# Delta-rule scan of a diffusion layer: two interleaved recurrences against one joint recurrence

## The chip, the cores and the metric

The kernel runs on one core of one Trainium2 chip, in one launch. The metric is the device time of that launch in microseconds (us); of several runs the median is taken. Four engines matter here: TensorE (PE, matmuls, with weight loads PEld beside them), VectorE (DVE), ScalarE (ACT), and the SyncE queue (SP) that issues most transfers. [...]

## The reference

One layer of a diffusion backbone over 512 latent tokens with 256 context tokens ahead, width 1024. A norm and one input projection feed two mixers, window attention and a bidirectional gated delta rule; their outputs are gated, summed, projected and added to the input, and an MLP follows. The change lies in the delta rule alone. Per direction (forward and backward in time), with 8 heads of 64 and chunks of 64 tokens:

```python
w_mat = triangular_solve(t_mat, (bc * eG)[..., None] * kc, ...)
u_v = triangular_solve(t_mat, bc[..., None] * vc, ...)
intra = dec_incl * jnp.einsum('bhnid,bhnjd->bhnij', qc, kc)
q_dec = eG[..., None] * qc
k_tail = jnp.exp(g_last[..., None] - G)[..., None] * kc

def step(S, xs):
    w_c, uv_c, qd_c, intra_c, kt_c, gl_c = xs
    u = uv_c - jnp.einsum('bhck,bhkv->bhcv', w_c, S)
    o = jnp.einsum('bhck,bhkv->bhcv', qd_c, S) + jnp.einsum('bhij,bhjv->bhiv', intra_c, u)
    S = jnp.exp(gl_c)[..., None, None] * S + jnp.einsum('bhck,bhcv->bhkv', kt_c, u)
    return S, o
...
return o_f + flip(o_b), s_f, s_b
```

The context has 4 chunks and the latents 8. The context scan starts from zero, its states start the latent scan, and its outputs are not used.

## The kernel before, in words

Everything is fp32. Large matrices are split into a high and a low part (`split`, and lines 271 and 276 for weights: ACT makes the high part, DVE the low one), and each product is three fp32r matmuls of 128x512. The scan's own products are small plain fp32 matmuls, 64x64 by 64 columns, four of them side by side in quarters of the array. The profile counts each of these as two records.

The scan is slow in latency and small in work, so large products are laid between its pieces. They come from a generator `fill` (432 products of 128x512: eight tiles of `br_a`, line 1086, then gate tiles of `gate_tiles`, line 1040; each tile is a group in one PSUM bank that ACT drains at its end, through the helper at line 164 or at 1088). `run_fill(n)` lays n of them at a place, and `FILL` holds the counts. The program's order is only a priority: a planner puts each engine's instructions into a fixed order when the kernel is built, from its own estimate of when each becomes ready, so a product that is not ready in its estimate lets later ones pass. On the chip each engine then works strictly in that order, with semaphores for the dependencies.

`chain_step(d, step)` is one step of one direction. Its state `state[d]` is [128 x 256]: two heads on the two halves of the partitions, four pairs side by side. `zb[d]` is one pair of PSUM banks per direction, in which all products of that direction lie. A step has three pieces, and `steps` runs each piece for d = 0, then d = 1, and then yields:

1. state products, line 1156: k·S and, in the latents, q·S (32 records of each kind for the two directions together); then on DVE R = eG·(k·S) (line 1160) and R = -0.5·v + R (line 1161).
2. u = X·R, line 1175, where X is the inverse of the triangular matrix; DVE makes `uk` = tb·u (line 1181), the decay and beta on the key side; in the latents ACT copies u (`us`, line 1185) and makes `zq` = eG·(q·S), in four pieces of 64 columns (line 1187).
3. k·uk, line 1195, into the same banks; ACT scales the old state in four pieces (`se`, line 1205), DVE makes the new state `se` - k·uk (line 1206; line 1200 in the first step); in the latents IA·us (line 1213), and DVE adds up the output (line 1218 in the first half of the steps, 1220, 1221, 1223 and ACT's square 1222 in the second half).

With `FILL[3] = (8, 7, 3)`, 8 large products follow piece 1, 7 piece 2 and 3 piece 3 in the latent scan.

The stages around it, in order of time in the profiled run:

- the context scan (about 290 to 348 us): the four context steps are woven with the inversion of the latents' triangular matrices on DVE (lines 864 and 865), 144 large products, and `rest()` (norm of q, line 676, and the token-major copies of k and v of the latents: `to_tokens`, four TensorE transposes at line 923 and ACT copies of 64x256 at line 928).
- the stage between the scans (about 348 to 398 us): the latents' inverses are completed (`combine`, lines 885 to 909), and the masked q·k blocks `IA` are made (line 786, DVE 1293 to 1296, ACT 1302 to 1305; `qq` takes two banks), with large products and with 12 pieces of `late_mod` between them: each loads 512 KB (`wada2`, line 1104) and reduces it on DVE (line 1105).
- the latent scan (about 398 to 470 us), with four more pieces of `late_mod`, each in a buffer that is taken for it from the arena.
- then the output norm of the scan (lines 1336 and 1341), the last gate tiles, the projections and the MLP.

Buffers in SBUF come from one arena of 167 units that is handed out in turn, so where a buffer lies, and what it has to wait for, depends on all that was taken before.

Of the kernel before, what the change touches and what calls it, by code (L numbers as in the profile page):

```python
# [20 lines left out]
FILL = 144, 28, 36, (8, 7, 3)  # L21
# [91 lines left out]
def tile_layer(ctx: ExitStack, tc: tile.TileContext, I: dict, out: bass.AP, dbg=None):  # L113
# [37 lines left out]
    bc = lambda ap, n: ap.unsqueeze(2).broadcast_to([ap.shape[0], ap.shape[1], n])  # L151

# [591 lines left out]
    eg = const.tile([P, 5, NM], F32, name="eg")  # L744
    eG, tb, tbO = eg[:, 0:2], eg[:, 2:4], eg[:, 4]
# [8 lines left out]
    act(eg[:, 0:5].rearrange("p n m -> p (n m)"), egp[:, :5 * NM], AF.Exp)  # L754
# [158 lines left out]
    def strided(ap, *dims):  # L913

        return bass.AP(ap.tensor, ap.offset, [list(ap.ap[0]), *map(list, dims)])

    def tok_major(src, dst, cs, places):

        hi, lo = (places[2] ^ places[0], places[1] ^ places[0])
        for c0 in cs[::2]:  # L920
            pt = bank()
            for q in range(4):
                PE.transpose(pt[:, q * P:(q + 1) * P], src[q][:, col(c0):col(c0) + P], ident)
            for i in range(2):
                o = (c0 + i - cs[0]) * 256
                for a in range(2):
                    sg = 64 - 128 * a
                    A.activation(dst[64 * a:64 * a + 64, o:o + 256].rearrange("p (x y f) -> p x y f", x=2, y=2),  # L928
                                 strided(pt[64 * i:64 * i + 64, 64 * a:512], (256 + sg * hi, 2), (128 + sg * lo, 2), (1, 64)), AF.Copy)
            pt.free()  # L930

    KTM, VTM = [None] * 3, [None] * 3
# [79 lines left out]
    def to_tokens(dst, src, g):  # L1012
        dst[g] = alloc(1024, True)
        tok_major(src, dst[g], range(4 * g, 4 * g + 4), ZP if dst is VTM else UP)
# [77 lines left out]

    for q in range(4):
        silu2(qT[q].ap, qT[q].ap)
# [5 lines left out]
    def late_mod(grp):  # L1100

        for j in range(8):
            wa = alloc(1024)
            nc.sync.dma_start(out=wa.ap, in_=I["wada2"][grp, j])
            V.scalar_tensor_tensor(wa.ap, wa.ap, 0.5, scr.ap, op0=ALU.mult, op1=ALU.mult, accum_out=modT[:, grp, j:j + 1])  # L1105
            wa.free()
            if j == 7:
                V.tensor_tensor(modT[:, grp], modT[:, grp], bada[:, 16 + 8 * grp:24 + 8 * grp], op=ALU.add)
            yield

    late = (x for grp in range(4) for x in late_mod(grp))
# [20 lines left out]
    hv = lambda ap: ap.rearrange("p (q v) -> p q v", q=4)  # L1132
    state = [None, None]
    zb = [bank(2), bank(2)]
    Sb = [[alloc(256), alloc(256)] for _ in range(2)]

    def chain_step(d, step):
        lat = step >= NCC
        c = step if d == 0 else NC_ - 1 - (step - NCC) if lat else NCC - 1 - step
        cl = c - NCC if lat else c  # L1140
        S, last = state[d], step == NC_ - 1
        m4 = slice(c * 4, c * 4 + 4)
        z = zb[d]
        r2 = [slice(0, 64), slice(64, 128)]
        vt = VTM[c // 4][:, c % 4 * 256:(c % 4 + 1) * 256]

        zt = z.ap.rearrange("p (b n) -> p b n", b=2)
        by2 = lambda ap: ap.rearrange("p (b n) -> p b n", b=2)
        hv2 = lambda ap: ap.rearrange("p b (q v) -> p b q v", v=HD)
        bc2 = lambda ap: ap.rearrange("p (b q) -> p b q", b=2).unsqueeze(3).broadcast_to([P, 2, 2, HD])  # L1150
        if S is not None:
            for x, src in enumerate((kT, qT) if lat else (kT,)):
                for q in (0, 2, 1, 3):
                    for a in range(2):
                        o = 512 * ZP[q] + 128 * x + 64 * (q % 2)
                        PE.matmul(z[r2[a ^ ZP[q]], o:o + HD], src[q][r2[a], col(c):col(c) + CH],
                                  S[r2[a], SPOS[q] * HD:(SPOS[q] + 1) * HD], start=True, stop=True)
            Rb = alloc(256)
            R = Rb.ap
            V.tensor_tensor(hv2(by2(R)), hv2(zt[:, :, 0:128]), bc2(eG[:, d, m4]), op=ALU.mult)  # L1160
            V.scalar_tensor_tensor(R, vt, -0.5, R, op0=ALU.mult, op1=ALU.add)
        else:
            R = vt
        yield
        u = zt[:, :, 256:384]

        def place(q):

            o = 512 * (UPOS[q] // 2) + 256 + 64 * (UPOS[q] % 2)
            return slice(o, o + HD)  # L1170

        for q in (0, 1, 3, 2):
            for a in range(2):
                r = r2[a ^ ZP[q]]
                PE.matmul(z[r2[a ^ UP[q]], place(q)], XA[lat][d][r, (cl * 4 + q) * CH:(cl * 4 + q + 1) * CH],
                          R[r, q * HD:(q + 1) * HD], start=True, stop=True)
        if S is not None:
            Rb.free()
        if not last:
            uk = alloc(256)  # L1180
            V.tensor_tensor(hv2(by2(uk.ap)), hv2(u), bc2(tb[:, d, m4]), op=ALU.mult)
        if lat:
            us, zqb = alloc(256), alloc(256)
            zq = zqb.ap
            A.activation(by2(us.ap), u, AF.Copy)
            for q in range(4):
                A.activation(zq[:, UPOS[q] * HD:(UPOS[q] + 1) * HD], zt[:, ZP[q], 128 + 64 * (q % 2):192 + 64 * (q % 2)], AF.Copy,
                             scale=eG[:, d, c * 4 + q:c * 4 + q + 1])
        yield
        if not last:  # L1190
            sn = zt[:, :, 384:512]
            for q in range(4):
                for a in range(2):
                    r, o = r2[a ^ UP[q]], 512 * UP[q] + 384 + 64 * (q // 2)
                    PE.matmul(z[r2[a], o:o + HD], KTM[c // 4][r, (c % 4 * 4 + q) * HD:(c % 4 * 4 + q + 1) * HD],
                              uk[r, UPOS[q] * HD:(UPOS[q] + 1) * HD], start=True, stop=True)
            uk.free()
            Sn = Sb[d][step % 2]
            if S is None:
                V.tensor_scalar(by2(Sn.ap), sn, 0.5, None, op0=ALU.mult)  # L1200
            else:
                se = alloc(256)
                for q in range(4):
                    o = slice(SPOS[q] * HD, (SPOS[q] + 1) * HD)
                    A.activation(se[:, o], S[:, o], AF.Copy, scale=egl[:, d, c * 4 + q:c * 4 + q + 1])
                V.tensor_tensor(by2(Sn.ap), by2(se.ap), sn, op=ALU.subtract)
                se.free()
            state[d] = Sn
        if lat:
            for q in (0, 1, 3, 2):  # L1210
                for a in range(2):
                    r = r2[a ^ UP[q]]
                    PE.matmul(z[r2[a ^ ZP[q]], place(q)], IA[d][r, (cl * 4 + q) * CH:(cl * 4 + q + 1) * CH],
                              us[r, UPOS[q] * HD:(UPOS[q] + 1) * HD], start=True, stop=True)
            us.free()
            dst = ot_[:, cl * 256:(cl + 1) * 256]
            if step - NCC < NCL // 2:
                V.tensor_tensor(by2(dst), by2(zq), u, op=ALU.add)
            else:
                V.tensor_tensor(by2(zq), by2(zq), u, op=ALU.add)  # L1220
                V.tensor_tensor(dst, dst, zq, op=ALU.add)
                A.activation(zq, dst, AF.Square)
                V.tensor_reduce(oss[:, cl], hv(zq), axis=AX.X, op=ALU.add)
            zqb.free()

    def steps(r):
        for step in r:
            both = [chain_step(d, step) for d in range(2)]
            for _ in range(3):
                for g in both:  # L1230
                    next(g, None)
                yield

    def rest():
        for q in range(4):
            l2n(qT[q].ap, HD ** -0.5, ((0, SEQ),), epsc4)
            yield
        for g in (1, 2):
            to_tokens(VTM, vT, g)
            yield  # L1240
        for t in vT:
            t.free()
        for g in (1, 2):
            to_tokens(KTM, kT, g)
            yield

    to_tokens(VTM, vT, 0)
    to_tokens(KTM, kT, 0)
    weave((steps(range(NCC)), 3 * NCC), (inv, 40), (fill, FILL[0]), (rest(), 9))
    for _ in inv:  # L1250
        pass
    for b in KTM[:1] + VTM[:1] + XA[0]:
# [59 lines left out]

    ot_ = alloc(2048, True)
    ot = ot_.ap.rearrange("p (c q v) -> p c q v", c=NCL, q=4)
    for n, _ in enumerate(steps(range(NCC, NC_))):
        run_fill(FILL[3][n % 3])
        if n % 3 == 1 and n < 3 * NCL // 2:
            run_late(1)
    for _ in fill:
        pass  # L1320
    for b in kT + qT + KTM[1:] + VTM[1:] + XA[1] + IA + zb + Sb[0] + Sb[1]:
# [362 lines left out]
def pack(i):  # L1684
# [45 lines left out]
    for n, (kind, places, order) in enumerate(((0, ZP, range(4)), (1, ZP, range(4)), (0, UP, UORD), (1, UP, UORD), (0, (0,) * 4, range(4)))):  # L1730
# [27 lines left out]
```

## Time and profile before

| | us |
|---|---|
| median of 3 runs | 913.39 (912.81 to 914.12) |
| the profiled execution | 911.42 |
| span of its profile | 909.7 |
| TensorE busy in it | 873.9 (96%) |
| VectorE busy | 652.9 (72%) |
| ScalarE busy | 496.9 (55%) |

The span runs from the first to the last instruction; 1.7 us of the execution lie outside it. TensorE's matmuls overlap each other, so its busy time is the time in which at least one runs, and the mean duration of a matmul is not what the next one waits.

### The profile page before, as it was taken

The page shows a single profiled execution, that of the slowest core. Times are in us where ns is not written, and L with a number is a line of the kernel's source. Part 1 is how long each engine was busy: PE and PEld are TensorE (multiplying, and loading weights), DVE is VectorE, ACT ScalarE, POOL GpSimd, SP SyncE. Part 2 cuts the span into 40 slices and gives each one's busy share as a digit, 9 for nine tenths or more (in the row PEclk, how much of TensorE's full clock was granted, in tenths as well). Part 3 has the DMA queues.
Part 4 walks back from the last instruction along what each step waited for, and adds up shares of the span by engine and source line. Part 5 has one row for each costly group of instructions (what it writes and reads, how often), then busy time and mean ns, then how long its engine had stood idle before and what let it go on. Part 6 is the DMA issues. An engine that isn't in the chain of part 4 may idle for free.

```text
span 909.7 us, 18033 instructions
## 1 busy us (share of the span) xinstructions
PE 873.9 (96%) x7564; PEld 721.3 (79%) x7564; DVE 652.9 (72%) x1111; ACT 496.9 (55%) x881; POOL 26.0 (3%) x42
## 2 busy tenths in 40 slices
PE   8999999989999998889999999999999999999998
PEld 6688667867777676656677789888898899889986
DVE  5665799876778999566666968896587567837631
ACT  6368764475768795475654434463265246424520
POOL 0000001010000001100000000000000000000000
PEclk9999999999999999999999999999999999999999
DMA  9824455532311136523143645453412332334031
GB/s 355 312 76 117 94 131 107 113 73 47 57 36 35 59 121 235 182 67 99 49 152 107 241 127 186 155 170 115 139 48 93 116 116 70 116 93 139 1 116 46
DMA packets 31985, 107.13 MB, mean 118 GB/s; under 512 B 4000, under 2 KB 4512, under 8 KB 31904
## 3 DMA queue, kind: packets, MB, share of 16 engines
q1 hardware_dynamic: 29600, 97.59, 32.1%
q0 software_dynamic: 2304, 8.39, 5.8%
q8 instruction: 59, 0.97, 0.4%
q14 instruction: 22, 0.18, 0.1%
HBM read 103.87 MB, written 2.10 MB: 116 GB/s over the span
## 4 chain that ended last, share of the span: by engine, by line
PE 60%; DVE 20%; ACT 11%; DMA 6%; issue 3%; SPq 0%; ACTq 0%; DVEq 0%
PE banks L293 12%; PE banks L294 12%; PE banks L295 12%; PE banks L1509 11%; PE banks L1040 5%; DMA m<-in_wada 3%; ACT m L164 2%; DVE m L865 2%; DVE m L864 2%; DVE m L1105 2%; DVE m L204 2%; DMA m<-in_wm 1%; DVE wl L276 1%; ACT m L928 1%; DVE m L875 1%
## 5 line engine op out<-in xcount | busy, mean ns | idle before, releaser
L293 PE MATMUL banks<-m,wh 128*128 128x512 f32 (+1 forms) x568 | 213.2, 376 | 0.5 <-ACT m L203 0.5
L294 PE MATMUL banks<-m,wh 128*128 128x512 f32 (+1 forms) x568 | 210.7, 371 | 0.3 <-DVE m L204 0.2
L295 PE MATMUL banks<-m,wl 128*128 128x512 f32 (+1 forms) x568 | 209.8, 370 | 0.0
L271 ACT ACTIVATE wh<-wr 128x1024 fp32r<-128x1024 f32 (+1 forms) x92 | 90.6, 987 | 130.5 <-PE banks L294 102.5
L1509 PE MATMUL banks<-m,m 128*128 128x256 f32 x1008 | 123.2, 284 | 0.9 <-ACT m L203 0.6
L1509 PEld LDWEIGHTS banks<-m,m 128*128 128x128 f32 x1008 | 121.9, 192 | 2.4 <-ACT m L203 1.2
L203 ACT ACTIVATE m<-m 128x512 fp32r<-128x512 f32 (+2 forms) x118 | 81.9, 719 | 75.0 <-DVE m L1487 12.0
L293 PEld LDWEIGHTS banks<-m,wh 128*128 128x128 f32 x568 | 107.0, 189 | 19.2 <-ACT m L203 1.0
L294 PEld LDWEIGHTS banks<-m,wh 128*128 128x128 f32 x568 | 107.0, 188 | 18.8 <-DVE m L204 1.2
L295 PEld LDWEIGHTS banks<-m,wl 128*128 128x128 f32 x568 | 106.9, 188 | 18.6 <-issue 0.7
L1040 PE MATMUL banks<-m,wh 128*128 128x512 f32 x320 | 108.2, 409 | 3.5 <-ACT m L164 3.5
L204 DVE TENSOR_TENSOR m<-m,m 128x512 fp32r<-128x512 f32 (+2 forms) x118 | 92.3, 804 | 22.3 <-ACT m L203 14.1
L276 DVE TENSOR_TENSOR wl<-wr,wh 128x1024 fp32r<-128x1024 f32 (+1 forms) x76 | 84.2, 1110 | 14.9 <-ACT wh L271 12.6
L1636 DVE SCALAR_TENSOR_TENSOR m<-banks,modT,m 128x512 f32<-128x512 f32 x32 | 24.0, 750 | 68.6 <-PE banks L295 68.4
L1040 PEld LDWEIGHTS banks<-m,wh 128*128 128x128 f32 x320 | 59.6, 190 | 16.5 <-ACT m L164 4.0
L1040 PE MATMUL banks<-m,wl 128*128 128x512 f32 x160 | 65.5, 410 | 0.0
L1105 DVE SCALAR_TENSOR_TENSOR m<-m,m 128x1024 f32<-128x1024 f32 x32 | 38.8, 1220 | 14.3 <-DMA m<-in_wada 14.2
L293 PE MATMUL banks<-m,m 128*128 128x256 f32 (+1 forms) x136 | 44.9, 344 | 1.4 <-ACT m L300 1.2
L294 PE MATMUL banks<-m,m 128*128 128x256 f32 (+1 forms) x136 | 45.1, 340 | 0.9 <-DVE m L301 0.8
L295 PE MATMUL banks<-m,m 128*128 128x256 f32 (+1 forms) x136 | 44.6, 337 | 0.0
L164 ACT ACTIVATE m<-banks,st 128x512 f32<-128x512 f32 (+1 forms) x32 | 23.5, 738 | 24.7 <-DVE st L570 24.4
L1040 PEld LDWEIGHTS banks<-m,wl 128*128 128x128 f32 x160 | 30.5, 190 | 6.5
(258 smaller groups left out, 1339.5 us busy)
## 6 DMA issues: line engine op xcount, KB each, us to landing
m<-in_wada SPq DMA_DIRECT2D x48, 512.0 KB, 5.3
wr<-in_wm SPq DMA_DIRECT2D x40, 512.0 KB, 3.6
wr<-in_win SPq DMA_DIRECT2D x39, 512.0 KB, 3.7
m<-in_wm SPq DMA_DIRECT2D x24, 512.0 KB, 3.9
wl<-in_win POOLq DMA_DIRECT2D x16, 512.0 KB, 5.6
m<-in_xT SPq DMA_DIRECT2D x8, 512.0 KB, 5.6
wr<-in_wbr SPq DMA_DIRECT2D x16, 256.0 KB, 2.6
wr<-in_wout SPq DMA_DIRECT2D x8, 512.0 KB, 3.8
```

The source lines that it names most:

```text
L164: r = A.activation(out_, in_, func, **kw)
L203: A.activation(r32(hi), src, AF.Copy)
L204: (eng or V).tensor_tensor(r32(lo), src, hi, op=ALU.subtract)
L271: upper[0] = A.activation(r32(hi), raw, AF.Copy)
L276: V.tensor_tensor(r32(lo), raw, hi, op=ALU.subtract)
L293: PE.matmul(acc, w[0][:, k, :], xhi, start=(start and i == 0), stop=False)
L294: PE.matmul(acc, w[0][:, k, :], xlo, start=False, stop=False)
L295: r = PE.matmul(acc, w[1][:, k, :], xhi, start=False, stop=(stop and i == n - 1))
L1040: PE.matmul(acc.ap, w[x][:, k, :], hx[k][y], start=(k == p == 0), stop=(k == KT - 1 and p == 2))
L1105: V.scalar_tensor_tensor(wa.ap, wa.ap, 0.5, scr.ap, op0=ALU.mult, op1=ALU.mult, accum_out=modT[:, grp, j:j + 1])
L1509: PE.matmul(dst, r32(self.w[w][i][:, k * P:(k + 1) * P]), xs7[x][k][j], start=(n == 0), stop=(n == 11))
L1636: V.scalar_tensor_tensor(xn_[ct], accs[ct].ap, modT[:, 3, ct:ct + 1], xn_[ct], op0=ALU.mult, op1=ALU.add)
```

## The change

Both directions become one recurrence, with 512 columns where there were 256.

- `scan_step` takes the place of `chain_step`: each product is issued for both directions, then one DVE or ACT instruction works on both. The state is one [128 x 512] buffer.
- The banks of the scan go by kind of product: a pair for k·S, a pair for u and the k·u products, and in the latent scan a third pair for q·S and the intra products. That is six banks in the latent scan, where there were four.
- tb (decay and beta of the key side) is multiplied into the token-major keys ahead of the scan: `k_tokens` makes a forward and a backward copy of each group of four chunks, each by one DVE multiply of 128x1024. So `uk` is gone; ACT's copy `us` of u is now made in every step and is what the k·u product reads.
- The 0.5 of v goes into the copies of v (`tok_major(..., scale)`); the output sums of a step (`sums`) are put off to the next step, behind its R. q·S moves behind u. `se` is made ahead of u; in the latents the backward half of it by one DVE multiply.
- The keys' copies for the latents move from the context scan into the stage between the scans (one group in each of the two `IA` rounds). The latents' v copies now come first in `rest()`.
- eG is written in the order of the steps (three small ACT exponentials in place of a part of one).
- The `late_mod` pieces of the latent scan share one buffer (`lbuf`); a few buffers are freed half way through the scan. `FILL[3]` is (8, 3, 7).

The core of the diff:

```diff
-FILL = 144, 28, 36, (8, 7, 3)
+FILL = 144, 28, 36, (8, 3, 7)
...
+    def k_tokens(g):
+
+        kf, kb = alloc(1024, True), alloc(1024, True)
+        tok_major(kT, kb, range(4 * g, 4 * g + 4), UP)
+        kv = lambda b: b.ap.rearrange("p (n f) -> p n f", f=HD)
+        for d, dst in ((0, kf), (1, kb)):
+            V.tensor_tensor(kv(dst), kv(kb), bc(tb[:, d, 16 * g:16 * g + 16], HD), op=ALU.mult)
+        KTM[g] = kf, kb
...
         for j in range(8):
-            wa = alloc(1024)
+            wa = lbuf[0] if lbuf else alloc(1024)
...
+    def sums(step, cl, zq, o):
...
+        if step - NCC < NCL // 2:
+            V.tensor_tensor(dst, by_d(b2(zq.ap)), by_d(o), op=ALU.add)
+        else:
+            V.tensor_tensor(b2(zq.ap), b2(zq.ap), o, op=ALU.add)
+            V.tensor_tensor(dst, dst, by_d(b2(zq.ap)), op=ALU.add)
+            A.activation(by_d(b2(zq.ap)), dst, AF.Square)
+            V.tensor_reduce(...)
+
+    def scan_step(step):
...
+        if S is not None:
+            with_state(kz, kT)
+            Rb = alloc(512)
+            V.tensor_tensor(heads(b2(Rb.ap)), heads(kz[:, :, 0:256]),
+                            eGs[:, step]..., op=ALU.mult)
+            V.tensor_tensor(rv, rv, strided(v0, (128, 2), (vstep, 2), (1, 128)), op=ALU.subtract)
...
+        for f in later:
+            f()
+        later.clear()
+        if S is not None and not last:
+            se = alloc(512)
+            for d in range(1 + (not lat)):
+                for q in range(4):
+                    A.activation(se[:, o:o + HD], S[:, o:o + HD], AF.Copy, scale=egl[...])
+            if lat:
+                V.tensor_tensor(half(se.ap), half(S.ap), strided(egl[...]), op=ALU.mult)
         yield
+        for d in range(2):
+            ... PE.matmul(uz[...], XA[lat][d][...], R(d, q)[r], start=True, stop=True)
+        us = alloc(512)
+        A.activation(b2(us.ap), uz[:, :, 0:256], AF.Copy)
         if lat:
+            oz, zq = b2(zb[2].ap), alloc(512)
+            with_state(oz, qT)
+            for d in range(2):
+                for q in range(4):
+                    A.activation(zq[...], oz[...], AF.Copy, scale=eGs[...])
         yield
         if not last:
+            ... PE.matmul(uz[r2[a], UP[q], o:o + HD], KTM[cs2[d] // 4][d][r, k0:k0 + HD], u_(d, q)[r], ...)
+            Sn = Sb[step % 2]
+                V.tensor_tensor(b2(Sn.ap), b2(se.ap), uz[:, :, 256:512], op=ALU.subtract)
+        yield
         if lat:
+            ... PE.matmul(oz[r2[a ^ ZP[q]], b, 256 + o:256 + o + HD], IA[d][...], u_(d, q)[r], ...)
+            later.append(lambda: sums(step, cl, zq, oz[:, :, 256:512]))
...
     for g in range(2):
...
         run_late(LATE)
+        k_tokens(1 + g)
         run_fill(FILL[2] - FPAUSE)
```

More of the change, by code (lines that the diff above doesn't have):

```diff
@@ L1109, in late_mod @@
             yield
+    lbuf = []
     late = (x for grp in range(4) for x in late_mod(grp))
@@ L1131, in tile_layer @@
     oss = small([P, NCL, 4], "oss", bufs=1)
-    hv = lambda ap: ap.rearrange("p (q v) -> p q v", q=4)
-    state = [None, None]
+    state = [None]
     zb = [bank(2), bank(2)]
[L1135 to L1152, printed above, removed]
+    Sb = [alloc(512), alloc(512)]
@@ L1167, in place @@
[L1167 to L1176, printed above, removed]
+                        o = 128 * d + 64 * (q % 2)
+                        so = 256 * UP[q] + 128 * d + 64 * (q // 2)
@@ L1189, in chain_step @@
         yield
         if not last:
[L1191 to L1198, printed above, removed]
+            for d in range(2):
+                for q in range(4):
+                    for a in range(2):
+                        r, o = r2[a ^ UP[q]], 256 + 128 * d + 64 * (q // 2)
+                        k0 = (cs2[d] % 4 * 4 + q) * HD
+                        PE.matmul(uz[r2[a], UP[q], o:o + HD], KTM[cs2[d] // 4][d][r, k0:k0 + HD], u_(d, q)[r], start=True, stop=True)
@@ L1207, in chain_step @@
                 se.free()
-            state[d] = Sn
+            state[0] = Sn
+        yield
         if lat:
[L1210 to L1224, printed above, removed]
+            for d in range(2):
+                for q in (0, 1, 3, 2):
+                    for a in range(2):
+                        r, (b, o) = r2[a ^ UP[q]], place(d, q)
+                        PE.matmul(oz[r2[a ^ ZP[q]], b, 256 + o:256 + o + HD], IA[d][r, (cl[d] * 4 + q) * CH:(cl[d] * 4 + q + 1) * CH],
+                                  u_(d, q)[r], start=True, stop=True)
@@ L1226, in steps @@
+            later.append(lambda: sums(step, cl, zq, oz[:, :, 256:512]))
+        us.free()
     def steps(r):
         for step in r:
[L1228 to L1232, printed above, removed]
+            yield from scan_step(step)
     def rest():
+        yield from v_tokens(range(NCC, NC_))
+        for t in vT:
+            t.free()
+        yield
         for q in range(4):
@@ L1237, in rest @@
             yield
[L1238 to L1249, printed above, removed]
+    for _ in v_tokens(range(NCC)):
+        pass
+    k_tokens(0)
+    weave((steps(range(NCC)), 3 * NCC), (inv, 40), (fill, FILL[0]), (rest(), 7))
     for _ in inv:
         pass
-    for b in KTM[:1] + VTM[:1] + XA[0]:
+    for b in [*KTM[0], VTM[0], *XA[0]]:
         b.free()
@@ L1311, in tile_layer @@
     dump("qT0", qT[0].ap)
+    for b in kT:
+        b.part(SEQ, CTX).free()
+    lbuf.append(alloc(1024))
     ot_ = alloc(2048, True)
-    ot = ot_.ap.rearrange("p (c q v) -> p c q v", c=NCL, q=4)
+    zb.append(bank(2))
+    first = [b.part(1024 * d, 1024) for bs in (XA[1], IA) for d, b in enumerate(bs)] + [KTM[1][0], KTM[2][1]]
     for n, _ in enumerate(steps(range(NCC, NC_))):
+        if n == 3 * NCL // 2:
+            for b in first:
+                b.free()
         run_fill(FILL[3][n % 3])
```

102 lines of the change are left out of this document (64 added, 38 removed).

## The prediction

> **What bounds the kernel now.** I read the page's busy times first, then the busy time by stage, then, for the latent scan alone, the groups by line and shape, the waits, and TensorE's timeline.
>
> ```profile
> span 909.7 us, 18033 instructions
> PE 873.9 (96%) x7564; PEld 721.3 (79%) x7564; DVE 652.9 (72%) x1111; ACT 496.9 (55%) x881; POOL 26.0 (3%) x42
> ```
>
> TensorE is busy nearly always: 909.7 - 873.9 = 35.8 us is all that filled gaps could ever give. By stage (context scan, the stage between, latent scan, the rest; columns are length, then busy time of PE, PEld, DVE, ACT, POOL):
>
> ```profile
> 290.00:348.00 58.00, 55.02 (x557) 41.16 (x556) 54.90 (x104) 47.39 (x107) 2.07 (x4) 0.97 0.29 92
> 348.00:398.00 50.00, 43.60 (x970) 33.83 (x968) 34.91 (x58) 26.98 (x49) 5.76 (x12) 1.00 0.56 191
> 398.00:470.00 72.00, 66.58 (x1319) 46.97 (x1319) 45.73 (x105) 45.94 (x156) 0.46 (x1) 1.00 0.22 69
> 470.00:910.00 440.00, 432.58 (x2511) 381.99 (x2510) 298.40 (x440) 186.75 (x258) 0.00 (x0) 1.00 0.36 119
> ```
>
> The change's own stages leave 3.0, 6.4 and 5.4 us of TensorE idle. In the context scan DVE is 95% full, in the latent scan neither DVE nor ACT is (64% each). So instructions saved on them don't count there by their busy time, only by what TensorE waits for. But busy time hides a second loss. The latent scan, line by line:
>
> ```profile
> L1040 PE MATMUL banks<-m,wh 128*128 128x512 f32 x90 | 33.0, 420 | 0.0
> L1040 PE MATMUL banks<-m,wl 128*128 128x512 f32 x45 | 19.1, 425 | 0.0
> L1187 ACT ACTIVATE m<-banks,eg 128x64 f32<-128x64 f32 x64 | 15.0, 339 | 0.0
> L1156 PE MATMUL banks<-m,m 64*64 64x64 f32 x448 | 10.0, 223 | 0.7 <-DVE m L1218 0.4 <-DVE m L1220 0.2
> L1195 PE MATMUL banks<-m,m 64*64 64x64 f32 x224 | 9.3, 230 | 1.6 <-ACT m L1187 1.2
> L1175 PE MATMUL banks<-m,m 64*64 64x64 f32 x256 | 7.2, 229 | 2.7 <-DVE m L1161 2.5
> L1213 PE MATMUL banks<-m,m 64*64 64x64 f32 x256 | 6.7, 226 | 0.4 <-DVE m L1206 0.4
> L1160 DVE TENSOR_TENSOR m<-banks,eg 128x256 f32<-128x256 f32 x15 | 6.3, 419 | 1.1 <-PE banks L1156 1.1
> L1206 DVE TENSOR_TENSOR m<-m,banks 128x256 f32<-128x256 f32 x14 | 5.8, 419 | 12.8 <-PE banks L1195 10.8 <-ACT m L1187 1.9
> L1105 DVE SCALAR_TENSOR_TENSOR m<-m,m 128x1024 f32<-128x1024 f32 x3 | 3.7, 1226 | 2.7 <-DMA m<-in_wada 2.7
> L1296 DVE TENSOR_TENSOR m<-m,banks 128x512 f32<-128x512 f32 x1 | 0.7, 689 | 0.0
> ```
>
> That is 135 large products and 448 + 224 + 256 + 256 = 1184 records of small ones. Their undisturbed pace stands in the chain of work just after the scan, and in TensorE's timeline (start, length):
>
> ```profile
> 469.79 9.75 PE banks L1040 x42
> ```
>
> ```profile
> 398.15 0.46 PE L1175 MATMUL banks<-m,m 64*64 64x64 f32 x16
> ...
> 440.75 0.97 ACT L1187 ACTIVATE m<-banks,eg 128x64 f32<-128x64 f32 x4
> 441.17 1.05 PE L1195 MATMUL banks<-m,m 64*64 64x64 f32 x32
> 442.16 0.50 PE L1040 MATMUL banks<-m,wl 128*128 128x512 f32 x1
> 442.59 0.69 PE L1213 MATMUL banks<-m,m 64*64 64x64 f32 x32
> 443.21 0.73 PE L1040 MATMUL banks<-m,wh 128*128 128x512 f32 x2
> 444.36 1.02 PEld L1156 LDWEIGHTS banks<-m,m 64*64 64x64 f32 x64 [0.39 <-DVE m L1220]
> ...
> 446.03 0.62 PE L1040 MATMUL banks<-m,wh 128*128 128x512 f32 x2
> ...
> 469.10 0.69 PE L1213 MATMUL banks<-m,m 64*64 64x64 f32 x32
> ```
>
> A large product every 9.75/42 = 0.232 us, a small record every 1.02/64 = 0.016 us. 135 x 0.232 + 1184 x 0.016 = 31.3 + 18.9 = 50.2 us, and the stage is 72. Of the other 21.8 us the named waits of TensorE are 2.5 + 1.2 + 0.4 + 0.4 + 0.2 = 4.7. The rest is mostly the change between large and small products. Take the group at 442.59: from the large product ahead of it to the one behind it 443.21 - 442.16 = 1.05 us, less one product (0.232) and 32 records (0.51): 0.31 us; and the pair behind it took 0.73, where the pair at 446.03, with large ones around it, took 0.62. I call it 0.4 us a group, an estimate. From 398.15 to 469.10 I count 36 such groups in the timeline: 14.4 us. The remaining 2.7 us are stalls inside groups, like the 1.05 us at 441.17 for 32 records that take 0.69 two lines below: its second half waited for ACT's zq pieces (440.75, 0.97 us, so until 441.72).
>
> **The change part by part.**
>
> Groups in the latent scan. As programmed both kernels have three groups of small products a step: k·S behind the intra products of the step before, u (with q·S in the new one), and k·u. The old one ran 36 in 8 steps, 4.5 a step, because products of one direction weren't ready and large ones passed. In the new one all products of a group become ready by one instruction for both directions. At best 8 x 3 = 24 are left (-12 x 0.4 = -4.8 us), at worst 36 (0). I take 28, nearer to the best, since the pieces' readiness is now common but q·S and the intra products still have conditions of their own: -8 x 0.4 = **-3.2 us**.
>
> Waits in the latent scan. (a) L1195 waits for L1187, which reads other columns of the same banks, so the order is kept by bank; k·u therefore waited for all of zq. With q·S in a third pair this is gone: 1.2 us named, and 0.36 inside a group in up to 7 steps, 3.7 us at most. (b) L1175 <- L1161, 2.5 us: DVE's R. Part of it is R queued behind L1105, which itself waits for its transfer (2.7 us in this stage). The shared buffer lets each of those transfers start as soon as the one before is used, a step earlier; I credit half, 1.2. (c) New: R of both directions is now two instructions in a row. 256 columns take 419 ns, 512 take 689 (L1296), so R is ready 2 x 0.69 = 1.4 us after k·S, with about 0.1 for the hand-over; behind k·S lie 8 large products, 1.86 us, and half a change. That covers it by about 0.5 us while DVE is free, and not when a 1.23 us instruction (such as L1105) has just begun: then 0.6 us is bare. Say in two of eight steps, 1.2 us. (d) New: q·S must wait until the output sum of the step before has left the third pair of banks; that is one DVE instruction of 0.69 behind R, while u's group lasts 0.51: 0.2 x 8 = 1.6 us. What is queued behind q·S on TensorE is the large products and k·u. The new state (0.69 us on DVE, and 0.42 less for `uk` ahead of it) lies behind 7 products and the intra group, 2.1 us. Sum: -3.7 - 1.2 + 1.2 + 1.6, about **-2.0 us**; between -6 (all waits gone, 4.7 named and part of the stalls) and +3 (c bare in every step).
>
> [...]
>
> Context scan. TensorE's waits there include u's consumer:
>
> ```profile
> PE banks L1195 <- DVE m L1181: 1.7, 2, 1.2
> PE banks L1040 <- ACT m L164: 2.9, 2, 2.3
> L928 ACT ACTIVATE m<-banks 64x256 f32<-64x256 f32 x48 | 18.1, 377 | 0.6
> L1088 ACT ACTIVATE m<-banks 128x512 f32<-128x512 f32 x8 | 4.7, 586 | 0.0
> ```
>
> (the first two rows are of the waits from 290 to 480 us, the others of the groups from 290 to 500). k·u no longer waits for DVE, whose queue held the inversion and transposes, but for an ACT copy of about 0.59 us (L1088). 1.7 us can go; ACT's own queue may take some of it: -1.2. DVE: of 27 instructions of 0.42 (11.3 us) become 6 for R and 4 for the state of 0.69 (6.9) and 2 key multiplies of about 1.23 (2.5, by L1105's width): -1.9 us of a full engine, but TensorE has only 3.0 us idle here and large products to run. ACT loses 16 of the 48 copies at L928 (-6.0) and gains four of `us` (+2.4). I take **-1.2 us**, between -3.0 and +1.
>
> The stage between. It takes in what the context scan loses: the keys' 16 transposes and 16 copies (6.0 us of ACT), and 4 key multiplies (4.9 us of DVE), behind `late_mod` on DVE. ACT's queue matters for one reason: the 2.9 us of L1040 <- L164 (longest 2.3) is a gate tile that wants a bank which ACT has not drained, because ACT was making IA:
>
> ```profile
> 391.31 0.41 ACT L1305 ACTIVATE m<-m 32x256 f32<-32x256 f32 x1
> 391.75 1.06 ACT L271 ACTIVATE wh<-wr 128x1024 fp32r<-128x1024 f32 x1
> 392.71 0.58 ACT L164 ACTIVATE m<-banks 128x512 f32<-128x512 f32 x1
> 393.34 0.72 PE L1040 MATMUL banks<-m,wh 128*128 128x512 f32 x2 [2.30 <-ACT m L164]
> ```
>
> The scan then holds four banks, `qq` two, and two are left; the transposes want one of these as well. Nothing to +2 x 3.0 us (ACT's copies ahead of a drain, once a round); nearest is one wait like the 2.3. I take **+1.7 us**. TensorE's share of the move costs nothing, the same 16 transposes leave the stage before.
>
> Small things. The last step's sums come behind the scan at 512 columns. L1336 is what the first output transpose waits for, after 42 large products that hide most of it; +0.3 (0 to +1). The three exponentials for eG, well before the scan, and the subtraction in place of L1161 at equal width: 0. Buffers move in the arena for the whole of the rest (432.58 of 440 us busy, so little to win): 0, ±1.5.
>
> Sum: -3.2 - 2.0 - 1.2 + 1.7 + 0.3 = **-4.4 us**. The profiled execution took 911.42 us (1.7 more than its span), 2.0 below the median 913.39; a stage's saving is the same in both, so 913.4 - 4.4 = **909.0 us**.
>
> **The rivals.**
>
> Lockstep (slower). Two recurrences covered each other: while DVE made R of one, TensorE had the other's products. Now every wait is common to both. Place: u's group behind R, in 11 steps. Price: when DVE is taken at the end of k·S, 0.6 us; with sums, splits and `late_mod` crowding into the same gaps, 0.6 us in each of 11 steps (6.6) and some 1.4 at the new state: -4.4 + 8 = +3.6, 917 us. It decides from the point where R comes later than 1.86 + 0.2 us after k·S in most steps. Against it: DVE's share in the latent scan falls (two of 256 cost 0.84, one of 512 0.69, and `uk` goes). For it: DVE's 95% in the context scan. Chance 0.18.
>
> Banks (no change). The wait for drained banks that costs 2.3 us once now comes in each IA round, and the scan keeps six banks, two for the gate tiles. +6 in place of +1.7: -0.1, 913 us. Against it in the scan itself: a tile of 24 products spans 24/135 of 72 us, 13 us, far longer than any stretch of ACT. Chance 0.17.
>
> [...]
>
> The planner splits the groups as before (gain without its first term): -4.4 + 3.2 = -1.2, 912.2 us. The groups at 1195 stood split with nothing but its estimate as a reason, and it still has conditions for q·S and IA. Chance 0.15.
>
> All of it works: 24 groups and nearly all named waits gone, -4.8 - 4.5 and the stage between for nothing: about -9, 904.4 us. Chance 0.08.
>
> **How the numbers follow.** The forecast has 0.42, with its own range 905 to 912. About 0.2% (1.8 us) is what a measurement can tell from no change. Faster by more: 0.39 of the forecast, all of the last rival 0.08, 0.06 of the split groups, 0.06 of the banks: 0.59. Within: 0.02, 0.07, 0.06 and 0.01 of lockstep: 0.16. Slower: 0.25, which is lockstep's 0.17, the bad ends of banks and split groups, and misplaced buffers. Range for 8 in 10: from 904, which takes in most of the full gain, to 917, lockstep's middle.
>
> **What the changed profile would show.** Right: the latent scan about 67 us in place of 72, some 28 groups of small products in it, no wait of k·u for zq; 512-column DVE instructions near 0.69 us, and `us` near 0.59; the stage between 1 to 2 us longer, with ACT ahead of the gate tile's drain. Wrong: u waiting for R in most steps (lockstep); L1040's successor waiting for drains by more than 5 us (banks); 36 groups again. A gain or a loss outside 290 to 480 us would be the arena's.

## The result and the profile after

The joint recurrence is slower: 916.66 us (median, 912.69 to 922.13) against 913.14 (911.01 to 915.10) for the kernel before, a ratio of 1.004, 95% interval 1.0027 to 1.0053. The forecast was 909.0. The profiled execution took 916.27 us, 4.85 more than that of before.

The top of the page after:

```profile
span 914.5 us, 17917 instructions
PE 869.9 (95%) x7564; PEld 720.8 (79%) x7564; DVE 650.3 (71%) x1053; ACT 492.7 (54%) x850; POOL 26.1 (3%) x42
```

TensorE has 4.0 us less busy time than before and the span is 4.8 us longer, so 8.8 us more of it is idle. The same four windows as in the prediction say where to look:

```profile
290.00:348.00 58.00, 53.38 (x548) 39.36 (x548) 53.22 (x92) 44.68 (x97) 0.00 (x0) 1.00 0.31 94
348.00:398.00 50.00, 41.86 (x873) 32.92 (x871) 38.62 (x57) 31.13 (x56) 7.27 (x14) 0.93 0.57 191
398.00:470.00 72.00, 66.72 (x1452) 50.34 (x1442) 43.38 (x69) 43.16 (x129) 1.04 (x2) 1.00 0.24 75
470.00:914.00 444.00, 432.67 (x2505) 381.24 (x2503) 298.09 (x437) 185.38 (x256) 0.00 (x0) 1.00 0.36 117
```

In the latent scan TensorE is as busy as before (66.72 against 66.58) but runs 1452 records in place of 1319. The rest, which the change does not touch, is 4 us longer for the same busy time (432.67 against 432.58). To put times on this I compared the start of the k-th matmul that uses all 128 rows (4508 of them in both traces), after minus before. Between 300 and 470 us the two kernels run these matmuls in different orders, so single values mean nothing there:

| about (us) | 30 to 290 | 476 | 515 | 685 | 755 | 784 | 850 | 881 |
|---|---|---|---|---|---|---|---|---|
| after is late by | 2.3 | -1.4 | -1.4 | 0.6 | 1.1 | 4.0 | 4.8 | 4.9 |

Most of the first 2.3 us arise at 20 us, in a part that is the same in both (a stretch of half clock, see the last section). Between 290 and 515 us the change gains 3.7 us (2.3 + 1.4). Then 6.3 us are lost behind the scan (1.4 + 4.9), nearly all of it in the MLP. TensorE's largest waits from 640 us on, before and then after (the columns are total, times, longest):

```profile
PE banks L1509 <- ACT m L203: 0.6, 1, 0.6
PE banks L1509 <- DVE m L204: 0.3, 1, 0.3
PE banks L294 <- DVE m L204: 0.2, 1, 0.2
```

```profile
PE banks L1552 <- ACT m L207: 3.0, 4, 1.0
PE banks L297 <- ACT m L1563: 1.4, 1, 1.4
PE banks L1552 <- DVE m L208: 1.1, 2, 0.8
```

Lines 1509 and 1552 are the same products of the MLP. And the chain of waits in the worst place (start, length, what), before, where it is TensorE alone, and after:

```profile
751.89 16.20 PE banks L1509 x135
```

```profile
754.94 3.20 PE banks L1552 x26
758.14 0.02 issue
758.16 3.51 DMA m<-in_wm
761.67 0.02 issue
761.69 0.63 ACT m L207
...
765.17 1.46 ACT m L207 x2
766.63 0.49 ACT m L1563
...
767.16 0.50 PE banks L297
```

By this chain a transfer of raw MLP weights could start only at 758.14, when a product had read the buffer whose place it takes. The transfer took 3.51 us, the row of ACT's instructions behind it another 5.4 (761.69 to 767.12), and the product that needs them came late: from 755 to 785 us TensorE is busy for 27.73 of 30 us, before for all 30. The queue that issues these transfers shows it too, its waits for those products, before and after:

```profile
SPq L1482 <- PE banks L1509: 42.5, 7, 11.6
```

```profile
SPq L1525 <- PE banks L1552: 51.4, 13, 9.9
```

Why do places differ so far behind the scan? One cause is a buffer that is never given back. The context scan advances the generator of steps exactly 3 x 4 times; `scan_step` has code behind its third yield (`us.free()`), which the old step piece did not need for its last piece. So the 512-column `us` of the last context step holds two of the arena's 167 units to the end, and all that is taken later lies elsewhere.

### The profile page after: what moved, and what is told of

It is laid out like the page before. It is cut to its first block, busy times and chain, and to the rows that moved or that the text cites. A ratio compares the mean times of both kernels' runs of the same rounds, so it can differ in the third digit from the quotient of the medians.

```text
span 914.5 us, 17917 instructions
## 1 busy us (share of the span) xinstructions
PE 869.9 (95%) x7564; PEld 720.8 (79%) x7564; DVE 650.3 (71%) x1053; ACT 492.7 (54%) x850; POOL 26.1 (3%) x42
```

## The experiments

Theory A: the change gains in the scan, and the places of the buffers behind it cost more. Theory B: the scan itself, or the half clock, makes the kernel slower. Line numbers differ by a few between the kernels; in the runs with the places set by hand, the products of the MLP are lines 1563 and 1518, and line 1510 where two units are held.

**Scan and places crossed.** The new scan with the places of before, from the output projection on:

```diff
+    ctx_steps = steps(range(NCC))
-    weave((steps(range(NCC)), 3 * NCC), ...)
+    weave((ctx_steps, 3 * NCC), ...)
+    for _ in ctx_steps:
+        pass
...
-    Y = [alloc(1024) for _ in range(8)]
+    Y = [mem.claim(s, 1024) for s in (99, 103, 107, 115, 135, 139, 143, 147)]
+    mem.ptr = 151
```

(`claim` takes a buffer at a given unit; two earlier groups of buffers keep off these units.) The old scan with the places of after:

```diff
-    Y = [alloc(1024) for _ in range(8)]
+    mem.claim(34, 512)
+    Y = [mem.claim(s, 1024) for s in (80, 84, 88, 92, 96, 105, 115, 135)]
+    mem.ptr = 139
```

By the traces, TensorE, VectorE and ScalarE have from about 540 us on the order of instructions of the kernel whose places were given. The orders of before and after differ up to about 860 us, so in these runs the places bring their order with them.

> The changed kernel with two edits: the 512-column buffer that its context scan never hands back is handed back, and from the output projection on every buffer lies where the kernel before has it, so that the order of instructions there is the one of before. Theory A (the loss is made behind the scan, by where buffers lie and the order that follows from it; the scan itself gained): the MLP stage takes what it took before, the lead of some 3.7 us that the profile shows at the end of the scan stays, about 909 us (907 to 911). Theory B (the joint recurrence is slower in itself, or keeps TensorE's clock down): about 916 us as the changed kernel, and the MLP stage as long as in it.

> The mirror of the run above: the kernel before with its own scan, but from the output projection on with the buffers of the changed kernel, the two lost units included, and so with its order of instructions. Theory A: the MLP stage loses the 6 us or so that it loses in the changed kernel, about 919 us (917 to 921). Theory B: no change, 913 us.

Measured: the first 909.90 us, ratio to before 0.997 (0.9956 to 0.9984); the second 919.88, ratio 1.0087 (1.0056 to 1.0119). As a table of medians, with 912.41 for before in the first of these runs:

| | places of before | places of after |
|---|---|---|
| old scan | 912.4 | 919.9 |
| new scan | 909.9 | 916.7 |

The places cost 7.5 us with the old scan and 6.8 with the new one; the new scan gains 2.5 with the old places and 3.2 with the new ones. The 916.7 comes from other rounds, with 913.1 for before beside it; by the ratios the places cost 7.9 and 6.4 us, and the scan gains 2.7 and 4.3. The waits from 640 us on go with the places and not with the scan; first the new scan with old places, then the old scan with new ones:

```profile
PE banks L1563 <- ACT m L214: 1.2, 1, 1.2
PE banks L1563 <- DVE m L215: 0.3, 1, 0.3
```

```profile
PE banks L1518 <- ACT m L210: 3.4, 4, 1.0
PE banks L300 <- ACT m L1529: 1.4, 1, 1.4
PE banks L1518 <- DVE m L211: 1.1, 2, 0.9
```

That settles it for A: a loss larger than the gain, behind the scan, from the places and the order of instructions that the planner makes from them. How much of it is late transfers and how much is the other order, these runs do not show.

Theory B keeps a small part. The granted clock of every run is on record: its mean is 0.9916 over the 12 runs of the new scan with the old places, and 0.9950 over the 23 of before beside them. Within one kernel, a run whose clock is lower by 0.001 takes about 0.5 us longer (all runs taken together), so by this estimate some 1.8 us of the new scan's gain are lost again to half clock. The old scan with the new places has 0.9928, too near to 0.9950 to make its 7.5 us.

**The buffer alone.** The new kernel with that one buffer handed back (the first part of the diff above and nothing else), and the kernel before holding 512 columns that it does not use (`alloc(512)` behind the context scan):

> The changed kernel, with only the lost 512-column buffer handed back; all places behind it move, to yet another pattern. Theory A: the scan's lead stays and the MLP stage is any of the patterns: between 909 and 917 us, another time than 916.7 by more than 1 us. Theory B: 916.7 us within 1 us.

> The kernel before, with a 512-column buffer taken behind the context scan and never given back: nothing is computed with it, only places move. Theory A: another pattern behind the scan, so the time moves by more than 1 us, rather up (913 to 920 us). Theory B: 913 us within 1 us.

Measured: 912.79 us, ratio 1.000 (0.9985 to 1.0015), and 925.84, ratio 1.0148 (1.0123 to 1.0173). Handing it back wins 3.9 of the 6.8 us. The places are then neither those of before nor those of after, because the scan's other buffers differ too; that the rest comes from these is likely and was not tried. Holding two units costs the old kernel 13.4 us, with nothing of the scan changed:

```profile
PE banks L1510 <- ACT m L203: 7.1, 5, 3.1
```

```profile
SPq L1483 <- PE banks L1510: 92.3, 12, 18.2
```

Part of the 13.4 us is clock: this trace has 10.2 us of half clock in the MLP's stretch (755.8 to 759.2 and 854.8 to 861.6 us), where the trace of before has none; that is worth at most 5.1 us. The size of the loss is not a matter of how much memory is held: two units, 1.2% of the arena, move the old kernel by 13.4 us and the new one by 3.9.

**The scan itself.** The base is the new scan with the old places (909.90). Its trace shows three things to try: ACT's scaled old state waits 3.0 us for a place that DVE has just used; u waits for R 7 times, 5.1 us in all, of which 4 times and 2.7 us lie in the latent scan; the keys' transposes compete for two banks in the stage between. Four edits:

```diff
-            se = alloc(512)
+            if step == NCC:
+                se, mem.ptr = mem.claim(52, 512), 41
+            else:
+                se = alloc(512)
```

> Base: the new scan with the places of before behind it (909.9 us in its runs, 2.5 below before). There ACT's first copy of the latent scan, the scaled old state, waits 3.0 us for DVE's last modulation product, because its buffer lies on units 39 and 40 and that product's transferred rows lie on 37 to 40; the drain of a gate tile queued behind it comes late, TensorE waits 3.6 us for the drain, and a stretch of half clock (6.83 us) follows. This kernel gives that one buffer units 52 and 53, free since the stage before; nothing else moves. Theory A (places make waits inside the stage between the scans too): both waits go and perhaps the half clock with them, -2 to -6 us on the base, a ratio to before of 0.991 to 0.995. Theory B (the stage is bound by its transposes and the two banks left, the wait only shows where): another wait takes its place, within 1 us of the base, 0.996 to 0.998.

Measured: 911.81 us, ratio 0.9985 (0.9971 to 0.9998). A falls, and the time lies above B's range too. The wait of 3.6 us fell to 1.9, and another grew in the same stage from 1.3 to 6.4, the keys' transposes for the drained `qq`:

```profile
PE banks L934 <- DVE m L1341: 6.4, 1, 6.4
```

```diff
-FILL = 144, 28, 36, (8, 3, 7)
+FILL = 144, 28, 36, (8, 7, 3)
```

> Base as for e5. The large products between the groups of a latent step go back from 8, 3, 7 to 8, 7, 3: seven behind u, three behind the new state's products. Theory A (the waits decide, as the forecast's step on the new state has it): ACT's copy of u needs no more than 0.6 us and had cover enough with three; the new state (0.69 us on DVE, with the hand-over about 1 us) now has three products (0.70) and the intra group (0.5) as cover in place of seven and is bare by 0 to 0.4 us in up to 7 steps: +0.5 to +3 us on the base, ratio to before 0.998 to 1.001. Theory B (the number of groups decides, and the planner places the large products by its own costs): the number stays near 25 and the time within 1 us of the base, 0.996 to 0.998.

Measured: 910.19, ratio 0.9967 (0.9951 to 0.9983): B. Which of these two gaps is filled makes no difference that shows here.

The same line with (10, 3, 5):

> Base as for e5. Ten large products behind k.S in place of eight, five behind the new state in place of seven. In the base u waits for R 7 times, 5.1 us in all, 1.1 at most. Theory A (R of both directions is too long for eight products: the forecast's step c, bare in nearly every step rather than in two of eight): two more products are 0.46 us a step, u's wait falls to about 2 us and the new state is still covered: -2 to -3.5 us on the base, ratio to before 0.993 to 0.995. Theory B (the two products are missed elsewhere, the new state or the intra group becomes late by as much): within 1 us of the base, 0.996 to 0.998.

Measured: 907.93, ratio 0.9938 (0.9918 to 0.9958): at the edge of A's range. In the latent scan u's wait fell from 2.7 us to 1.6. (The expectation of (12, 3, 3) below sets 1.6 beside 5.1, which are of different stretches: over both scans it is 4.1 beside 5.1, and the context scan's part does not change.) So the wait gives 1.1 of the 2 to 3 us that were won.

```diff
-            later.append(lambda: sums(step, cl, zq, oz[:, :, 256:512]))
+            sums(step, cl, zq, oz[:, :, 256:512])
```

> Base as for e5. The output sums of a latent step are issued right behind its intra products, not behind the R of the step after. Theory A (order on DVE decides: the sum waits for the intra products and stands ahead of R): R comes later by the sum's 0.69 us in up to 7 steps, u waits by as much more, +2 to +5 us, ratio to before 0.999 to 1.003. Theory B (the planner puts R ahead anyway, or q.S gains what R loses, since the third pair of banks is drained sooner): within 1 us of the base, 0.996 to 0.998.

Measured: 910.20, ratio 0.9965 (0.9950 to 0.9980): B. Putting the sums off gains nothing that shows.

**Four more: the stage between, the scan's fill, and both.** First the keys of both rounds ahead of the first `qq`:

```diff
-        k_tokens(1 + g)
+        if g == 0:
+            k_tokens(1)
+            k_tokens(2)
```

> Base: the new scan with the places of before behind it (909.9 us). In its rounds of the stage between the scans, and in the changed kernel, the keys' transposes of the second round stand behind the first round's q.k products and want a bank that DVE has yet to read (4.5 us of wait in the changed kernel, 1.3 in the base, 6.4 in the run that gave the first scaled state another buffer). This kernel transposes the keys of both rounds ahead of the first round's pair of banks; the same instructions, the second half earlier. Theory A (two banks left in this stage hold TensorE up, the forecast's second rival): that wait goes, -1 to -4 us on the base, ratio to before 0.993 to 0.996. Theory B (ACT's 8 copies more in the first round hold up a gate tile's drain there, as the 3.6 us wait of the base does): within 1 us of the base or above it, 0.996 to 1.000.

Measured: 911.46, ratio 0.9979 (0.9966 to 0.9991): B. The transposes wait only 0.4 us now, but q·k waits 2.9 us for DVE and u waits for R by up to 2.1.

That edit and (10, 3, 5) together:

> The edit of e9 and that of e7 (10, 3, 5 large products between the groups of a latent step; 907.9 us by itself) together. Theory A (two waits of different stages): the gains add, 904 to 907 us, ratio to before 0.990 to 0.993. Theory B (the run with 10, 3, 5 gained in the stage between, where its trace had half clock for 3.41 us in place of 10.2, and not in the latent scan): e9's edit moves the same stretch, and the pair gives no more than the better one, 907.5 to 910.

Measured: 911.16, ratio 0.9973 (0.9959 to 0.9988): the gains do not add, as B says, and the time is above B's 907.5 to 910 too. Its interval lies just above that of (10, 3, 5) alone, so the edit takes back what that gained.

The base with (12, 3, 3) and nothing else:

> Base as for e9. Twelve large products behind k.S, three behind u, three behind the new state's products. In the run with 10, 3, 5 u waited for R 3 times, 1.6 us, against 7 times, 5.1 us, with 8, 3, 7. Theory A (R's cover is what counts): the wait goes altogether; with three behind the new state nothing was lost in the run with 8, 7, 3, so 906 to 908 us, ratio 0.992 to 0.995. Theory B (what 10, 3, 5 gained was chance of order in the stage before): anything within 2 us of the base, 908 to 912, ratio 0.995 to 0.999, though u waits less.

Measured: 907.41, ratio 0.9925 (0.9905 to 0.9946), in A's range, and the lowest time: it beats both kernels (913.46 for before beside it). From (10, 3, 5) it can't be told apart, since the two intervals overlap. TensorE's waits of u for R from 398 to 470 us, base and this kernel:

```profile
PE banks L1230 <- DVE m L1209: 2.7, 4, 0.9
```

```profile
PE banks L1230 <- DVE m L1209: 0.6, 2, 0.3
```

That is 2.1 us; a new wait of k·u for ACT's copy of u (1.5 us, once) gives most of it back. Half clock in the scan stages fell from 13.7 to 6.8 us in these two traces, worth at most 3.4 us, but the base's profiled execution is the slowest of its twelve. The clocks of all runs are the better measure: the base's mean of 0.9916 is 0.0034 below before's beside it, this kernel's 0.9938 (6 runs) is 0.0005 above before's 0.9933. At 0.5 us for 0.001 that is an estimated 2 us of the gain on the base (4.1 us by the two ratios). So A's number came, but not by R's cover alone; B's "chance" is not excluded as a part of it.

Last, (10, 3, 5) with `k_tokens(1 + g)` moved below `run_fill`:

> 10, 3, 5 as in e7, and in each round of the stage between the keys' transposes stand behind the round's large products, just ahead of its pair of banks. Theory A (two banks hold the stage up): the transposes come when the first round's pair has long been read, the wait of 1.9 us that e7's trace has for them goes, -1 to -2 us on e7, 906 to 907, ratio 0.992 to 0.993. Theory B (they then take a bank from the q.k products right behind them): within 1 us of e7 or above it, 907.5 to 910.

Measured: 909.14, ratio 0.9948 (0.9931 to 0.9965): B. The transposes now wait 6.1 us for ACT's drains, in place of 1.9 for DVE.

## Why the prediction was wrong

**The step that failed** is the last of the small things: "Buffers move in the arena for the whole of the rest (432.58 of 440 us busy, so little to win): 0, ±1.5". Its size is about +7 (6.8 and 7.5 in the crossed runs, 6.3 between the two traces), with the change of order that the places bring. A busy share bounds what can be won, and I used it as a bound on both sides. What can be lost was to be read elsewhere: the transfers of raw weights there wait for places (42.5 us of the queue's waits in before, up to 11.6 at once), take 3.5 us each and have 5 us of ACT's splitting behind them, so a transfer made late by a few us can bare TensorE; in the worst place of the trace after, for 2.3 of 30 us. The forecast's last sentence named the test: a loss outside 290 to 480 us would be the arena's. It was.

**The scan's terms** came out near their sum by luck: the latent scan gained 2.5 us more than forecast, the two other stages lost 1.6 and 1.7 us more, and these errors mostly cancel. In equal windows the work done can be counted: gate tiles' large products (0.232 us each), transposes (5.9 us busy for 46 in before, 0.13 each), and small records (0.016). The counts of before stand in the prediction for the latent scan; for the other two windows, before (context scan, then the stage between):

```profile
L1040 PE MATMUL banks<-m,wh 128*128 128x512 f32 x36 | 13.0, 442 | 0.0
L1040 PE MATMUL banks<-m,wl 128*128 128x512 f32 x19 | 8.1, 429 | 0.0
L923 PE MATMUL banks<-c_ident,m 128*128 128x128 f32 x46 | 5.9, 274 | 0.0
```

```profile
L1040 PE MATMUL banks<-m,wh 128*128 128x512 f32 x92 | 29.7, 398 | 2.9 <-ACT m L164 2.9
L1040 PE MATMUL banks<-m,wl 128*128 128x512 f32 x46 | 18.8, 409 | 0.0
L786 PE MATMUL banks<-m,m 64*32 64x64 f32 x256 | 3.7, 224 | 0.0
```

and after, in the same order and then the latent scan:

```profile
L1056 PE MATMUL banks<-m,wh 128*128 128x512 f32 x41 | 14.3, 421 | 0.0
L1056 PE MATMUL banks<-m,wl 128*128 128x512 f32 x21 | 8.2, 393 | 0.0
L927 PE MATMUL banks<-c_ident,m 128*128 128x128 f32 x30 | 4.2, 280 | 1.8 <-ACT m L1104 1.5 <-ACT m L932 0.4
```

```profile
L1056 PE MATMUL banks<-m,wh 128*128 128x512 f32 x81 | 27.7, 420 | 2.0 <-ACT m L168 2.0
L1056 PE MATMUL banks<-m,wl 128*128 128x512 f32 x40 | 16.9, 422 | 0.0
L927 PE MATMUL banks<-c_ident,m 128*128 128x128 f32 x16 | 2.9, 319 | 4.5 <-DVE m L1328 4.5
L794 PE MATMUL banks<-m,m 64*32 64x64 f32 x192 | 2.9, 224 | 0.0
```

```profile
L1056 PE MATMUL banks<-m,wh 128*128 128x512 f32 x107 | 37.3, 408 | 0.0
L1056 PE MATMUL banks<-m,wl 128*128 128x512 f32 x54 | 22.3, 413 | 0.0
L1188 PE MATMUL banks<-m,m 64*64 64x64 f32 x480 | 11.5, 221 | 1.0 <-DVE m L1250 0.4 <-DVE m L1328 0.4 <-DVE m L1164 0.2
L1223 PE MATMUL banks<-m,m 64*64 64x64 f32 x256 | 5.6, 224 | 2.8 <-DVE m L1202 1.9 <-ACT m L168 0.8
L1245 PE MATMUL banks<-m,m 64*64 64x64 f32 x224 | 4.9, 224 | 0.8 <-ACT m L1228 0.8
L794 PE MATMUL banks<-m,m 64*32 64x64 f32 x75 | 1.2, 224 | 0.0
```

- Latent scan, forecast -5.2 (groups -3.2, waits -2.0). In 72 us it runs 161 large products in place of 135 (6.0 us), 32 more records of k·S and q·S, and 75 of q·k that came in from the stage ahead (1.7): a gain of 7.7 us. From the first u on I count 23 groups of small products in the timeline, where the prediction counts 36: fewer than the 28 I took, at my best case. At the prediction's estimate of 0.4 us each these 13 are 5.2, which leaves about 2.5 for the waits. k·u no longer waits for zq, as forecast; it waits 0.8 for the copy of u. q·S waits 0.2 us, once, for the output sum, which reads other columns of the same banks (L1188 <- L1164), where I charged 1.6. u waits 1.9 us for R, where before waited 2.5 and the forecast had 2.5 again (1.2 won, 1.2 charged). Of the copies, 512 columns on DVE take 684 to 688 ns and `us` 593, as forecast.
- Stage between, forecast +1.7, between 0 and +6. It runs 17 large products fewer (3.9 us), 64 records of q·k and 32 of k·S fewer (1.5), and 16 transposes more (2.1): a loss of 3.3 us. The wait that came was not ACT ahead of a gate tile's drain (2.0 us now, 2.9 before) but that of the transposes. In TensorE's timeline and in DVE's:

```profile
389.35 1.11 PE L927 MATMUL banks<-c_ident,m 128*128 128x128 f32 x4 [4.55 <-DVE m L1328]
```

```profile
380.79 1.22 DVE L1029 TENSOR_TENSOR m<-m,eg 128x1024 f32<-128x1024 f32 x1
...
383.06 1.22 DVE L1029 TENSOR_TENSOR m<-m,eg 128x1024 f32<-128x1024 f32 x1
...
384.80 1.22 DVE L1122 SCALAR_TENSOR_TENSOR m<-m,m 128x1024 f32<-128x1024 f32 x1
...
388.61 0.69 DVE L1328 TENSOR_TENSOR m<-m,banks 128x512 f32<-128x512 f32 x1
```

  The second round's transposes want a bank of `qq`, and DVE's last reading of it (388.61) stood in its queue behind two key multiplies, a modulation product and the instructions that mask `qq`. A stretch of half clock begins within that wait (last section); how the 3.3 us split between the two is not shown. I had the 4.9 us of key multiplies on DVE and the two banks that are left of the kernel's eight (line 133 of before), but not that the one holds up the other. The rival on banks had the right resource; its price (+6 in place of +1.7) was too high, and the runs that moved the transposes (0.9979 and 0.9948) show that another wait of that stage takes over.
- Context scan, forecast -1.2. Seven large products more (1.6 us) for 16 transposes fewer (2.1): a loss of 0.5, so nothing was gained there: k·u's wait of 1.7 us for DVE is gone, but u waits 2.5 us for R in place of 0.8. It is worse than it looks, since before's trace has 3.3 us of half clock in this window (0.97 in its row) and after's has none.
- The last sums behind the scan, forecast +0.3, cost nothing that shows: the first output transpose waits 0.8 us, before 1.0.
- Together -7.7 + 3.3 + 0.5 = -3.9 us (-3.7 by the starts of the matmuls), against -4.4 forecast. By the medians the scan gains 2.5 to 3.2.

The rival on lockstep gave the right sign and, with 917 us, nearly the measured time, but by luck. Its sign did appear: u waits for R in 6 of 11 steps, 4.4 us in all. That is only about 1 us more than before's 3.3, against the 6.6 charged for it, and the latent scan is faster. That the wait is real fits the two best times, those with ten and twelve products behind k·S.

## What to carry to other kernels

Where a planner orders instructions and buffers are handed out in turn, an edit reaches all that comes later: look for what can be lost in the slack of the later transfers, not in the idle time of the busy engine, and before judging an edit give the later buffers back their places. Count who still holds a buffer at the end of a generator; one advanced a fixed number of times never runs what stands behind its last yield. In this kernel's stage with two free banks, each of the four runs that moved buffers or transposes there only changed which wait is last.

## What the runs showed of the hardware

In the traces of before and after the granted clock falls to 0.50 in stretches of 3.41 us (before, at 344.7 us) and of twice that, 6.83 us (after, at 19.8 and at 388.4 us), apart from one at the end of each that runs past the last instruction. In before's stretch the large products start 0.43 us apart (345.26 and 345.69 us), ahead of it 0.23 (340.15 and 340.38). Where the stretches fall differs between executions of equal parts. After has the one at 19.8 us in an unchanged part, where before's profiled execution has none; it explains most of the 2.3 us at the start (2.1 of them arise between 20 and 30 us). After's other one, 388.4 to 395.3 us, begins 3.6 us after the start of the 4.55 us wait above, with TensorE idle for all of the 3.4 us ahead of it, and is the 0.93 in the window from 348 to 398. TensorE works again from 389.35, so it costs at most half of the 5.9 us left, 3.0. In before, the 3.4 us ahead of the stretch at 344.7 us:

```profile
341.30:344.70 3.40, 1.79 (x36) 1.46 (x37) 3.40 (x6) 3.29 (x6) 1.55 (x3) 1.00 0.26 107
```

TensorE was busy for 1.79 of 3.40 us, with no single wait over 1.22. Ahead of the stretch at 19.8 us in after TensorE was busy for 1.8 of 3.4 us too. But in before it was busy for 1.8 of the 3.4 us up to 18.25 us and for 1.1 of the 3.4 us up to 393.35, and the clock stayed at 1.00 in the 3.4 us behind either, so what makes a stretch begin is not settled here.
